# Four-layer hybrid decoder trunk: giving dense blocks out by recently streamed columns, merging over all columns, and moving one gate tile

## The chip, the cores and the metric

The kernel runs on one core of one Trainium2 chip, as one launch. The metric is the device time of a launch in microseconds, the median of three runs; the profile is of one further execution. Engines are named as the profile names them: PE (TensorE matmuls), PEld (its weight loads), DVE (VectorE), ACT (ScalarE), POOL (GpSimd) and SP (SyncE, which issues all DMAs here).

## What is computed

16 learned meta tokens and 256 tokens of width 1024 pass through four layers. Each layer is a token mixer and a SwiGLU FFN (inner width 2816), each added to the residual after an RMS norm. The mixers are, in order, forgetting attention (FoX, 16 heads of 64), gated linear attention (GLA, 4 heads), gated DeltaNet (8 heads of 128) and FoX again. Everything is fp32. The two mixers that matter here, cut to their cores:

```python
def fox_attend(q, cq, qpos, k, v, ck, kpos):
    s = jnp.einsum('bqhd,bkhd->bhqk', q, k)
    s = jnp.where(kpos[None, :] <= qpos[:, None], s + cq[..., :, None] - ck[..., None, :], -jnp.inf)
    return jnp.einsum('bhqk,bkhd->bqhd', jax.nn.softmax(s, axis=-1), v)

def gdn_chunk(state, inputs):
    ...
    lower = jnp.einsum('bhtd,bhsd->bhts', kb, kh) * jnp.exp(jnp.where(strict, diff, -jnp.inf))
    t_mat = jnp.eye(C) + lower
    sol = lax.linalg.triangular_solve(t_mat, rhs, left_side=True, lower=True, unit_diagonal=True)
    ...
```

After the DeltaNet's chunks each head's output is normed and multiplied by `silu(gate)`, then projected by `w_out`.

## The kernel before

Activations lie transposed, features on partitions and the 272 tokens as columns, in eight tiles of 128 features. A **dense block** is a 128x128 piece of a weight matrix times one such tile. Each fp32 operand is split in two fp32r parts (`wh`, `wl` of a weight; `zh`, `zl`, `ah`, `al`, `oh`, `ol` of an activation), and a block is three fp32r matmuls of 272 columns: `block`, L551. Eight blocks are a **weight unit**: `make_unit` (L573) issues its DMA on SP's queue, ACT copies it to `wh`, DVE subtracts to get `wl`; three units are held. An output tile of a mixer's input projection is eight blocks, one unit, 24 matmuls; the order of tiles is also the order of units in the packed weight array (`pack_weights`, `_in_cols`). Everything that is not dense (norm sums, scores, solves) is plain fp32 matmul, which the profile shows as two records each.

The order of work is made by a **planner**, the class `Trunk`, which runs in Python while the program is built and gives every engine its instruction order. It keeps its own clock `now` for PE. Tasks are generators; at a `yield` of tiles a task sleeps until the planner expects these tiles, and a `yield` of an event until it is set. `turn` (L470) picks what PE does next: if `warm` is false, dense blocks come first (`step`, L506); otherwise the first task that is ready, and a dense block only when no task is. `step` takes blocks of up to three open output tiles, whose weight units must be among the three held, and opens the next tile in a fixed order when a PSUM bank is free; it stops at a tile whose event is not set. `pe` (L398) records each PE instruction, advances `now` and, at the end of each planner tick (`TICK`, 3.413 us), sets `warm` by the columns counted in the tick (`> 3060`); while it is not warm an instruction is costed at double. `mm` (L412) counts an fp32 matmul as four times its columns, times the share of 128 rows that it uses, and an fp32r matmul as its columns times that share; it issues the instruction at L419. `tr` (L422) issues transposes at L424. PE instructions keep the planner's order on the chip; so if PE is sent an instruction whose operand isn't there yet, everything behind it waits. DVE, ACT and POOL instructions are placed by `Lane` (L260 in the profile).

**FoX, `attend` (L932).** One call per pair of heads, eight per FoX layer. It takes four PSUM banks for the scores, applies the softmax on DVE and ACT (`sm`, `mn`, `pr`, `su`, `ri`), transposes the probabilities on PE, copies them out (ACT to `pts`, DVE to `pt2`), and multiplies them with `vsb` into the bank `po`; ACT copies `po` to `osb`, which the gate task (`gate_done`, L1009) waits for. Between the second head's transposes and the matmuls of `po` (L993) the task does not pause.

**DeltaNet, `gdn` (L1328).** The 33 input tiles follow `GDN_ORDER` (L34): keys `k` 0 to 7, gates `r` 0 to 4, queries `q` 0 to 3, values `v` 0 and 1, `r` 5 to 7, `v` 2 and 3, then `q` and `v` 4 to 7 (a tile with decay and beta comes ahead of them). Tiles from place 19 on, other than gates, wait for `in_ev` (L1750). That event is set by `inverse` (L1517): a substitution of 15 steps on DVE (`tmp`, `gx`), transposes and copies give the inverses of 16x16 diagonal blocks of the chunk's triangle, `xm` and `xt`. `merge` (L1558) joins these to inverses of the whole chunk, for 4 heads and one of three chunks (96, 96 and 80 tokens) per call: first pairs of 16-blocks into 32-blocks, then 32 into 64 and 64 into the chunk, each step a few small fp32 matmuls with an ACT or DVE operation between. The three calls of heads 0 to 3 run first, then those of heads 4 to 7. In the first step only the half of the columns that can change is computed (`half`, L1570), 48 of 96 or 32 of 64, both products in one PSUM bank. `solve(i)` (L1676) waits for its head's merges, query and value, at most three heads at once; `wrap`, `gated` and `out_norm` follow, then the output projection. A gate tile `r` is evicted by DVE to `sr`, goes through Silu on ACT (`r_done`, L1737) and is read by `gated` after its head's solve.

Of the kernel before, what the change touches and what calls it, by code (L numbers as in the profile page):

```python
# [9 lines left out]
F32R = mybir.dt.float32r  # L10
# [23 lines left out]
GDN_ORDER = (  # L34
    [("k", i) for i in range(8)]
    + [("r", i) for i in range(5)]
    + [("q", i) for i in range(4)]
    + [("v", i) for i in range(2)]
    + [("r", i) for i in range(5, 8)]
    + [("v", i) for i in range(2, 4)]  # L40
    + [(c, i) for c in "qv" for i in range(4, 8)]
)
OUT_WIDE = 6
KEPT = ("_const_", "_z_", "_wraw_", "_wsp_", "_ps_")

# [33 lines left out]
def out_order(kind):  # L79

    if kind != "gdn":
        return [(i, k) for i in range(KD) for k in range(KD)]
    return [
        (i, k)
        for i0, i1 in ((0, OUT_WIDE), (OUT_WIDE, KD))
        for k0 in (0, KD // 2)
# [24 lines left out]
class Cols:  # L111

    def __init__(self):
        self.parts, self.at, self.n = [], {}, 0
# [193 lines left out]
class Trunk:  # L309
# [4 lines left out]
    RAWS = 3  # L314
    LAT = 0.14
    TICK = 3.413

    def __init__(self, tc, io, pcols, ccols, layers):
        self.tc, self.nc, self.io = tc, tc.nc, io
        self.pcols, self.ccols, self.layers = pcols, ccols, layers  # L320
        self.v = Lane(self, self.nc.vector, 0.1, 1 / 960.0)
        self.s = Lane(self, self.nc.scalar, 0.13, 1 / 1200.0)
        self.g = Lane(self, self.nc.gpsimd, 0.1, 2.4 / 1000.0)
        self.written, self.last, self.held = {}, {}, {}
        self.oh, self.ol, self.oh_ready = [None] * KD, [None] * KD, False
        self.issued, self.loaded, self.read, self.ended = 0.5, 0.0, [0.0] * self.RAWS, [0.0] * self.WBUFS
        self.now, self.seq = 0.0, 0
        self.tick, self.cols, self.warm = 0, 0, False
        self.tasks, self.bg, self.open = [], [], []
        self.banks, self.freed = 0, []  # L330
        self.nblock, self.units, self.nunit, self.used, self.first = 0, {}, 0, {}, 0
        self.prev = None
        self.begun, self.late, self.taken, self.epoch = set(), [], [], 0.0
# [64 lines left out]
    def pe(self, ins, cost, cols, aps, ready):  # L398
        if self.prev is not None:
            self.behind(ins.ins, self.prev)  # L400
        self.follow(ins.ins, aps, self.prev)
        self.prev = ins.ins.name
        self.now = max(self.now, ready)
        tick = int(self.now / self.TICK)
        if tick != self.tick:
            self.warm = tick == self.tick + 1 and self.cols > 3060
            self.tick, self.cols = tick, 0
        self.cols += cols
        self.now += cost if self.warm else 2 * cost
        self.touch(aps[0], self.now + 0.07, True)  # L410

    def mm(self, out, lhsT, rhs, start=True, stop=True, share=1.0):  # L412
        n = out.free_size()
        if lhsT.dtype == F32R:
            cost = max(0.1, n / 2400.0 + 0.003)
        else:
            n *= 4
            cost = max(0.07 + 0.0009 * lhsT.free_size(), n / 2400.0 + 0.003) * share
        ins = self.nc.tensor.matmul(out, lhsT, rhs, start=start, stop=stop)  # L419
        self.pe(ins, cost, n * rhs.shape[0] / 128, (out, lhsT, rhs), max(self.done_at(lhsT), self.done_at(rhs)) + self.LAT)  # L420

    def tr(self, out, in_):  # L422
        n = in_.shape[0]
        ins = self.nc.tensor.transpose(out, in_, self.con("ident")[:n, :n])  # L424
        self.pe(ins, 0.11, n, (out, in_), self.done_at(in_) + self.LAT)

    def go(self, gen):
        self.tasks.append([self.now, self.seq, gen, None])
# [41 lines left out]
    def turn(self):  # L470

        soon = []
        if not self.warm and self.step(soon):
            return True
        for t in self.tasks:
            at, ev = t[0], t[3]
            if ev is not None:
                if ev.t is None:
                    continue
                at = max(at, ev.t)  # L480
            if at > self.now:
                soon.append(at)
                continue
            try:
                r = next(t[2])
            except StopIteration:
                self.tasks.remove(t)
                return True
            t[0], t[3] = self.now, None
            if isinstance(r, Ev):  # L490
                t[3] = r
            elif isinstance(r, float):
                t[0] += r
            else:
                for a in r if isinstance(r, tuple) else (r,):
                    t[0] = max(t[0], self.done_at(a) + self.LAT)
            return True
        if self.step(soon):
            return True
        soon += [t for t in self.freed if t > self.now]  # L500
        if not soon:
            return False
        self.now = max(self.now, min(soon)) + 1e-6
        return True

    def step(self, soon):  # L506
        while True:
# [185 lines left out]
    def add_out(self, z, evs, nk, gain, lo=0, store=False, order=None):  # L693
# [17 lines left out]
        if order:  # L711
            places = {ik: self.nblock + n for n, ik in enumerate(order)}
            for i in range(KD):
                self.bg.append(Dense([places[i, k] for k in range(KD)], z, evs, lo, done(i), OUT_WIDE))
            self.nblock += KD * KD
# [112 lines left out]
    def fox(self, j, lo, gain):  # L828
# [9 lines left out]
        with ExitStack() as cx:  # L838
# [93 lines left out]
            def attend(jp):  # L932
# [10 lines left out]
                for hh in range(2):  # L943
                    r, hd = R[hh], 2 * jp + hh
# [24 lines left out]
                pts, pt2 = [], []  # L969
                for hh in range(2):  # L970
                    pt = yield from self.bank()
                    for i3, (a, b) in enumerate(qt):
                        for k3 in range(i3 + 1):
                            t0, n = TILES[k3]
                            src = pr[hh][: b - a, offs[i3] + t0 : offs[i3] + t0 + n]
                            if k3 == 0:
                                dst = pt[:n, a:b]
                            elif k3 == 1:
                                dst = pt[:n, T + a - 96 : T + b - 96]
                            else:  # L980
                                dst = pb[hh][:n, T : T + 80]
                            self.tr(dst, src)
                    x = tp.tile([96, 448], F32, tag="pts", name="pts")
                    x2 = tp.tile([80, 80], F32, tag="pt2", name="pt2")
                    s.activation(x[:, lo:], pt[:96, lo:448], AF.Copy)
                    v.tensor_copy(x2, pb[hh][:80, T : T + 80])
                    self.free(pt)
                    self.free(pb[hh])
                    pts.append(x)
                    pt2.append(x2)  # L990
                    if hh == 0:
                        yield pr[1]
                po = yield from self.bank()  # L993
                for i3 in range(3):
                    for hh in range(2):
                        r = R[hh]
# [331 lines left out]
    def gdn(self, j, lo, gain):  # L1328
# [5 lines left out]
        with ExitStack() as cx:  # L1334
# [223 lines left out]
            def merge(grp, i3):  # L1558

                yield in_ev  # L1560
                t0, n = TILES[i3]
# [3 lines left out]
                xtn, xmn, ymn = xtg[:n, :, :n], xmg[:n, :, :n], ym[:n, :, :n]  # L1565
                m = 16
                nn = n // 32 * 32
                nh = nn // 2

                def half(a, hf):  # L1570
                    return a[..., :nn].rearrange("p (n x c) -> p n x c", x=2, c=m)[:, :, hf, :]

                p = yield from self.bank()
                for i in range(4):
# [3 lines left out]
                    half_mask[:n, None, :n].to_broadcast([n, 4, n]), ALU.mult)  # L1578
                self.free(p)
                yield ym  # L1580
                p = yield from self.bank()
                for i in range(4):
                    self.mm(p[:n, i * 96 : i * 96 + nh], xtn[:, i], half(ymn[:, i], 0))
                    self.mm(p[:n, i * 96 + 48 : i * 96 + 48 + nh], ymn[:, i], half(xtn[:, i], 1))
                pv = p[:n, :384].rearrange("p (h x c) -> p h x c", h=4, x=2)
                for hf, a in ((0, xmn), (1, xtn)):
                    av = a[:, :, :nn].rearrange("p h (n x c) -> p h n x c", x=2, c=m)[:, :, :, hf, :]
                    sv = pv[:, :, hf, :nh].rearrange("p h (n c) -> p h n c", c=m)
                    v.tensor_tensor(av, av, sv, ALU.add)
                self.free(p)  # L1590
                yield xmg, xtg
                e2 = n - 64
                p = yield from self.bank()
                pv = p[:, :128].rearrange("p (h c) -> p h c", h=4)
# [5 lines left out]
                p = yield from self.bank()  # L1600
                pv = p[:, :128].rearrange("p (h c) -> p h c", h=4)
# [7 lines left out]
                p = yield from self.bank()  # L1609
                pv = p[:, :256].rearrange("p (h c) -> p h c", h=4)  # L1610
# [5 lines left out]
                p = yield from self.bank()  # L1616
                pv = p[:, : 4 * e2].rearrange("p (h c) -> p h c", h=4)
# [239 lines left out]
```

## Time and profile before

| what | us |
|---|---|
| median of 3 runs (1547.57 to 1555.5) | 1552.88 |
| the profiled execution | 1550.78 |
| its span, first to last instruction | 1549.0 |
| PE busy in it | 1498.8 |
| DVE busy, ACT busy | 1092.3, 781.8 |

The mean granted clock of PE over the span is 0.983; 1.00 is 2.4 GHz and 0.50 is 1.2 GHz. A busy time of PE counts a matmul from start to modelled end; since matmuls overlap, distances from start to start tell more than the mean duration of one. In windows, a number behind an engine is its busy time in the stretch, with the count of its instructions in brackets. The stages lie, in us: FoX 0 to 160, SwiGLU to 397, GLA to 540, SwiGLU to 745, DeltaNet to 969, SwiGLU to 1190, FoX to 1328, SwiGLU to the end.

### The profile page before, as it was taken

What the parts mean: (1) busy time and instruction counts of PE and PEld (TensorE: products, weight loads), DVE (VectorE), ACT (ScalarE), POOL (GpSimd) and SP (SyncE); (2) the same over time, 40 slices, a digit from 0 to 9 for tenths busy, and PEclk for the clock granted to TensorE, in tenths of its full rate; (3) what the DMA queues carried; (4) which work ended last, traced back from release to release, by engine and by line L of the source; (5) the groups of instructions that cost most, each with busy time, mean ns of one, the idle gap of its engine ahead of it and who ended that gap; (6) DMA issues with size and microseconds to landing.
All of it is one profiled execution on the core that took longest, in us unless ns stands there. A gap on an engine that the chain in (4) does not pass through costs nothing.

```text
span 1549.0 us, 29524 instructions
## 1 busy us (share of the span) xinstructions
PE 1498.8 (97%) x11985; PEld 1453.4 (94%) x11985; DVE 1092.3 (71%) x2161; ACT 781.8 (50%) x1418; POOL 18.1 (1%) x58
## 2 busy tenths in 40 slices
PE   7899999999999999999898998999999999999999
PEld 7888999999999999999897897999999888999999
DVE  7778776665796876655979476866656778786653
ACT  6556554444445544444675354544445556654442
POOL 0000000000000000000200000000000000000000
PEclk9999999999999999999998897999999999999999
DMA  5232455555433455555333021455554333455564
GB/s 192 98 107 96 156 178 175 177 177 177 145 102 106 144 187 168 175 178 175 112 122 109 21 86 65 161 178 172 177 172 163 110 111 108 136 191 189 184 199 138
DMA packets 63737, 225.25 MB, mean 145 GB/s; under 512 B 7232, under 2 KB 9632, under 8 KB 63600
## 3 DMA queue, kind: packets, MB, share of 16 engines
q1 hardware_dynamic: 63600, 223.36, 43.3%
q8 instruction: 94, 1.54, 0.4%
q14 instruction: 43, 0.35, 0.1%
HBM read 222.28 MB, written 1.05 MB: 144 GB/s over the span
## 4 chain that ended last, share of the span: by engine, by line
PE 82%; DVE 11%; ACT 4%; issue 1%; DMA 1%; SPq 0%; DVEq 0%; ACTq 0%
PE ps L419 82%; DVE wl L260 3%; ACT pr L260 1%; ACT wh L260 1%; DVE rq L260 1%; DMA w<-in_w_dram 1%; DVE pr L260 1%; DVE sm L260 1%; PE ps L424 1%; DVE k L260 1%; ACT pts L260 0%; DVE ri L260 0%; DVE yc L260 0%; SPq L392 0%; DVE d L260 0%
## 5 line engine op out<-in xcount | busy, mean ns | idle before, releaser
L419 PE MATMUL ps<-zh,wh 128*128 128x272 f32 (+1 forms) x2400 | 711.2, 296 | 8.2 <-ACT zh L260 6.8
L419 PE MATMUL ps<-zh,wl 128*128 128x272 f32 (+1 forms) x2400 | 693.4, 289 | 3.1 <-DVE wl L260 3.1
L419 PE MATMUL ps<-zl,wh 128*128 128x272 f32 (+1 forms) x2400 | 695.0, 290 | 0.0
L260 ACT ACTIVATE wh<-w 128x1024 fp32r<-128x1024 f32 x420 | 443.1, 1056 | 384.3 <-PE ps L419 191.6
L260 DVE TENSOR_TENSOR wl<-w,wh 128x1024 fp32r<-128x1024 f32 x420 | 512.2, 1221 | 161.4 <-ACT wh L260 161.1
L419 PEld LDWEIGHTS ps<-zh,wh 128*128 128x128 f32 x2400 | 456.6, 190 | 17.2 <-ACT zh L260 6.7
L419 PEld LDWEIGHTS ps<-zh,wl 128*128 128x128 f32 x2400 | 456.7, 190 | 6.0 <-DVE wl L260 4.4
L419 PEld LDWEIGHTS ps<-zl,wh 128*128 128x128 f32 x2400 | 456.3, 190 | 0.0
L419 PE MATMUL ps<-al,wh 128*128 128x272 f32 (+1 forms) x704 | 202.0, 287 | 0.0
L419 PE MATMUL ps<-ah,wl 128*128 128x272 f32 (+1 forms) x704 | 201.4, 286 | 0.0
L419 PE MATMUL ps<-ah,wh 128*128 128x272 f32 (+1 forms) x704 | 201.0, 285 | 0.0
L419 PEld LDWEIGHTS ps<-ah,wh 128*128 128x128 f32 x704 | 133.1, 189 | 0.0
L419 PEld LDWEIGHTS ps<-al,wh 128*128 128x128 f32 x704 | 132.4, 188 | 0.0
L419 PEld LDWEIGHTS ps<-ah,wl 128*128 128x128 f32 x704 | 132.2, 188 | 0.0
L260 DVE TENSOR_TENSOR s<-t,rs 128x272 f32<-128x272 f32 (+1 forms) x88 | 38.5, 437 | 64.9 <-ACT t L260 64.8
L260 DVE TENSOR_TENSOR al<-a,ah 128x272 fp32r<-128x272 f32 (+1 forms) x88 | 38.6, 438 | 64.4 <-ACT ah L260 64.3
L419 PE MATMUL ps<-oh,wh 128*128 128x272 f32 (+1 forms) x256 | 75.6, 295 | 1.2 <-ACT wh L260 1.2
L419 PE MATMUL ps<-oh,wl 128*128 128x272 f32 (+1 forms) x256 | 74.7, 292 | 1.0 <-DVE wl L260 0.9
L419 PE MATMUL ps<-ol,wh 128*128 128x272 f32 (+1 forms) x256 | 74.7, 292 | 0.1
L260 ACT ACTIVATE ah<-a 128x272 fp32r<-128x272 f32 (+1 forms) x88 | 36.8, 418 | 62.9 <-DVE a L260 62.9
L260 ACT ACTIVATE zh<-h,par 128x272 fp32r<-128x272 f32 x64 | 32.7, 519 | 67.7 <-DVE h L260 66.5
L260 ACT ACTIVATE pr<-sm,mn 96x192 f32<-96x192 f32 (+3 forms) x96 | 42.2, 441 | 26.3 <-DVE mn L260 26.2
(225 smaller groups left out, 1511.7 us busy)
## 6 DMA issues: line engine op xcount, KB each, us to landing
w<-in_w_dram SPq DMA_DIRECT2D x420, 512.0 KB, 3.3
h<-in_h_dram SPq DMA_DIRECT2D x4, 272.0 KB, 5.2
out_dram<-h SPq DMA_DIRECT2D x8, 128.0 KB, 3.3
mask<-in_fmask_dram SPq DMA_DIRECT2D x2, 210.0 KB, 5.0
con<-in_con_dram SPq DMA_DIRECT2D x1, 207.5 KB, 6.0
mask<-in_gmask_dram SPq DMA_DIRECT2D x1, 126.0 KB, 2.1
par<-in_par_dram SPq DMA_DIRECT2D x1, 87.5 KB, 3.1
half<-in_dmask_dram SPq DMA_DIRECT2D x1, 36.0 KB, 1.7
```

What stands on the lines that cost most here:

```text
L260: r = f(*args, **kw)
L419: ins = self.nc.tensor.matmul(out, lhsT, rhs, start=start, stop=stop)
L424: ins = self.nc.tensor.transpose(out, in_, self.con("ident")[:n, :n])
```

## The change

Five edits in one. (2) What `mm` and `tr` count is now weighted by the part of the 128x128 array that is used, and an fp32 matmul counts six times its columns rather than four. (3) `turn` gives dense blocks the first place not only when `warm` is false, but also when the work counted over the last tick's length of planner time is not above 2950. (4) `attend` pauses until the planner expects the copies of the transposed probabilities. (5) `merge` computes its first step over all columns, the two products in two PSUM banks; and gate tile 7 of the DeltaNet goes from its place behind `r` 6 to the end of the order.

```diff
-    + [("r", i) for i in range(5, 8)]
+    + [("r", i) for i in range(5, 7)]
     + [("v", i) for i in range(2, 4)]
     + [(c, i) for c in "qv" for i in range(4, 8)]
 )
+GDN_ORDER[31:31] = [("r", i) for i in range(7, 8)]
...
+    KEEP = 2950
+    NEAR = 2950
...
-            self.warm = tick == self.tick + 1 and self.cols > 3060
+            self.warm = tick == self.tick + 1 and self.cols > self.KEEP
             self.tick, self.cols = tick, 0
         self.cols += cols
+        self.recent = [x for x in self.recent if x[0] > self.now - self.TICK] + [(self.now, cols)]
...
     def mm(self, out, lhsT, rhs, start=True, stop=True, share=1.0):
         n = out.free_size()
+        work = n * rhs.shape[0] * lhsT.free_size() / 128**2 * (1 if lhsT.dtype == F32R else 6)
...
-        self.pe(ins, cost, n * rhs.shape[0] / 128, (out, lhsT, rhs), max(self.done_at(lhsT), self.done_at(rhs)) + self.LAT)
+        self.pe(ins, cost, work, (out, lhsT, rhs), max(self.done_at(lhsT), self.done_at(rhs)) + self.LAT)
...
-        self.pe(ins, 0.11, n, (out, in_), self.done_at(in_) + self.LAT)
+        self.pe(ins, 0.11, 2 * n * n * in_.free_size() / 128**2, (out, in_), self.done_at(in_) + self.LAT)
...
-        if not self.warm and self.step(soon):
+        if not self.busy() and self.step(soon):
             return True
...
+    def busy(self):
+
+        return self.warm and sum(c for t, c in self.recent if t > self.now - self.TICK) > self.NEAR
...
                     if hh == 0:
                         yield pr[1]
+                yield tuple(pts + pt2)
                 po = yield from self.bank()
...
-                p = yield from self.bank()
+                ps = yield from self.bankn(2)
                 for i in range(4):
-                    self.mm(p[:n, i * 96 : i * 96 + nh], xtn[:, i], half(ymn[:, i], 0))
-                    self.mm(p[:n, i * 96 + 48 : i * 96 + 48 + nh], ymn[:, i], half(xtn[:, i], 1))
-                pv = p[:n, :384].rearrange("p (h x c) -> p h x c", h=4, x=2)
+                    self.mm(ps[0][:n, i * 96 : i * 96 + nn], xtn[:, i], ymn[:, i, :nn])
+                    self.mm(ps[1][:n, i * 96 : i * 96 + nn], ymn[:, i], xtn[:, i, :nn])
                 for hf, a in ((0, xmn), (1, xtn)):
-                    av = a[:, :, :nn].rearrange("p h (n x c) -> p h n x c", x=2, c=m)[:, :, :, hf, :]
-                    sv = pv[:, :, hf, :nh].rearrange("p h (n c) -> p h n c", c=m)
+                    av, sv = (
+                        t[:, :, :nn].rearrange("p h (n x c) -> p h n x c", x=2, c=m)[:, :, :, hf, :]
+                        for t in (a, ps[hf][:n, :384].rearrange("p (h c) -> p h c", h=4)))
                     v.tensor_tensor(av, av, sv, ALU.add)
-                self.free(p)
+                    self.free(ps[hf])
                 yield xmg, xtg
```

## Rows read from the trace of the kernel before

**Rows 1.** The page: busy time of PE, and the chain that ended last by engine.

```profile
PE 1498.8 (97%) x11985; PEld 1453.4 (94%) x11985; DVE 1092.3 (71%) x2161; ACT 781.8 (50%) x1418; POOL 18.1 (1%) x58
...
PE 82%; DVE 11%; ACT 4%; issue 1%; DMA 1%; SPq 0%; DVEq 0%; ACTq 0%
```

**Rows 2.** Windows by stage: length, busy us and count per engine, granted clock, DMA share, GB/s.

```profile
0.00:160.00 160.00, 142.40 (x1109) 128.92 (x1109) 124.04 (x373) 92.41 (x228) 0.51 (x5) 0.99 0.37 123
160.00:397.00 237.00, 237.00 (x1881) 236.84 (x1881) 156.32 (x235) 114.13 (x164) 3.49 (x7) 1.00 0.52 174
397.00:540.00 143.00, 138.29 (x1130) 134.21 (x1129) 116.01 (x196) 75.82 (x130) 4.01 (x9) 1.00 0.37 121
...
745.00:969.00 224.00, 205.93 (x1598) 191.92 (x1597) 163.19 (x378) 117.71 (x267) 1.85 (x19) 0.89 0.25 82
...
1190.00:1328.00 138.00, 131.20 (x1061) 118.54 (x1060) 108.45 (x342) 80.76 (x208) 0.00 (x0) 1.00 0.33 110
```

**Rows 3.** Windows at changes of the granted clock, DeltaNet stretch (same columns).

```profile
849.55:856.37 6.82, 6.82 (x46) 6.27 (x45) 3.66 (x9) 2.88 (x6) 0.20 (x2) 0.50 0.00 0
887.10:897.33 10.23, 10.23 (x74) 8.97 (x72) 3.59 (x8) 3.50 (x9) 0.10 (x1) 0.50 0.22 72
934.89:948.50 13.61, 13.26 (x48) 11.38 (x49) 7.66 (x18) 5.98 (x20) 0.00 (x0) 0.50 0.24 78
...
846.10:849.50 3.40, 2.62 (x43) 2.56 (x44) 3.40 (x10) 2.09 (x6) 0.10 (x1) 1.00 0.02 5
883.70:887.10 3.40, 3.40 (x53) 2.99 (x53) 1.42 (x4) 0.79 (x3) 0.00 (x0) 1.00 0.02 5
...
926.00:934.90 8.90, 6.47 (x46) 5.26 (x45) 8.38 (x19) 5.12 (x12) 0.00 (x0) 1.00 0.19 60
```

**Rows 4.** Waits of PE, PEld, whole span: total us, times, longest us.

```profile
PE ps L419 <- ACT pts L260: 8.2, 16, 1.3
...
PE ps L419 <- DVE xm L260: 6.6, 1, 6.6
...
PE ps L419 <- DVE ym L260: 0.9, 1, 0.9
...
PEld ps L419 <- ACT pts L260: 15.6, 32, 1.8
```

**Rows 5.** Chain that ended last, DeltaNet stretch: start us, us, what.

```profile
830.81 0.44 DVE sr L260
...
837.39 6.93 PE ps L419 x42
...
846.88 20.59 PE ps L419 x202
...
894.62 25.23 PE ps L419 x182
```

**Rows 6.** Chain that ended last, end of the second FoX stretch.

```profile
1302.30 1.22 DVE wl L260
...
1322.38 0.42 ACT pts L260
```

**Rows 7.** PE's instructions by line and form, 900 to 928 us.

```profile
L419 PE MATMUL ps<-zh,wh 128*128 128x272 f32 x51 | 15.7, 307 | 0.0
```

**Rows 8.** Timeline of PE, merges at full clock: start us, us, instruction, count.

```profile
868.74 0.84 PE L419 MATMUL ps<-xm,l 96*96 96x96 f32 x8
...
871.38 0.33 PE L419 MATMUL ps<-xt,ym 96*96 96x48 f32 x2
...
872.40 0.33 PE L419 MATMUL ps<-xt,ym 96*96 96x48 f32 x2
```

**Rows 9.** Windows, end of the DeltaNet stretch (columns as in rows 2).

```profile
928.00:969.00 41.00, 35.65 (x194) 31.44 (x193) 27.31 (x62) 16.98 (x45) 0.00 (x0) 0.79 0.20 65
```

**Rows 10.** Timeline of PE, dense matmuls in the first slow piece (first and last of 15).

```profile
851.83 0.59 PE L419 MATMUL ps<-zh,wh 128*128 128x272 f32 x1
...
855.17 0.43 PE L419 MATMUL ps<-zl,wh 128*128 128x272 f32 x1
```

More of the change, by code (lines that the diff above doesn't have):

```diff
@@ L327, in __init__ @@
         self.now, self.seq = 0.0, 0
-        self.tick, self.cols, self.warm = 0, 0, False
+        self.tick, self.cols, self.warm, self.recent = 0, 0, False, []
         self.tasks, self.bg, self.open = [], [], []
@@ L1567, in merge @@
                 nn = n // 32 * 32
-                nh = nn // 2
-                def half(a, hf):
-                    return a[..., :nn].rearrange("p (n x c) -> p n x c", x=2, c=m)[:, :, hf, :]
                 p = yield from self.bank()
```

## The prediction

> **What bounds the kernel now.** The page comes first [rows 1]: the PE rows fill 97% of the span and the chain that ended last lies 82% on PE, so the question is where PE's order or clock wastes time. The windows by stage [rows 2] answer it: the first SwiGLU stretch has PE busy all of its 237 us at full clock (the other three look the same), while both FoX stretches leave PE idle (17.6 of 160 us, 6.8 of 138 us) and the gated-delta stretch, 745 to 969 us, is idle for 18.1 of 224 us at a granted clock of 0.89. Only these can give much back.
>
> In the delta stretch the windows show three long pieces at a granted clock of 0.50, half of 2.4 GHz [rows 3]: 849.55 to 856.37, 887.10 to 897.33 and 934.89 to 948.50 us. (A fourth follows the wait for the inverse's `xm`, 6.6 us [rows 4], and is due to that.) Ahead of the third PE was busy for only 6.47 of 8.90 us, waiting on solves. But the first two come out of small work: 846.10 to 849.50 us holds 43 matmuls and the wait of 0.9 us for `ym` [rows 4], 883.70 to 887.10 holds 53 and no idle time at all, most of them narrow merge matmuls. The clock fell there while PE had ready work. The chain [rows 5] runs through PE for 20.6 us from 846.88 on and again for 25.2 us from 894.62 on, so these two pieces cost real time: (6.82 + 10.23) / 2 = **8.5 us** against the same order at full clock.
>
> In FoX, PE waits for the copies `pts` 16 times, 8.2 us in all on the matmuls (15.6 us if the weight loads' waits are taken) [rows 4]. Each of the 16 `attend` calls gives out its output matmuls right behind the transposes, before the copy that they read is done; everything behind them in PE's order waits too.
>
> **The extra pause in attend (L993).** Nothing is added on the chip: the same instructions and semaphores, but the planner now hands PE other work until the copies are due. If there are dense blocks, the whole 8.2 us is filled; at most 15.6. But the end of a FoX stretch is not always PE's: from 1302 to 1322 us the second one's chain is DVE and ACT work, with the splits `wl` of 1.2 us among it [rows 6]. Time won before the last group's query and key tiles counts, what is won in the last group (2 of 8 calls) does not: 8.2 x 6/8 = **6.1 us**. Bounds 0 (the filling blocks wait for their own `wl` instead) and 15.6. What moves later is the output matmul, then `osb`, the gate and the output projection; in the body of a stretch nobody waits for these.
>
> **The new rule in turn (busy, recent, weights in mm and tr).** No work is added; dense blocks change places. Before, blocks came ahead of ready tasks only after a whole planner tick with few columns; now also when the last tick's length of planned PE work falls below 2950, where a narrow fp32 matmul counts little (a 32x32x32 one 12, against 32 before) and a full-width one counts 6 a column instead of 4. In the delta stretch that puts blocks between the merges, 843 to 900 us, in place of 900 to 928 us, where 153 dense records stand in one piece [rows 7]. A block is three matmuls 0.126 us apart (237 us hold 1881) [rows 2]. The nearest rows say what it earns: the first two pieces at clock 0.50, **8.5 us**. Below: 0, if the clock stays as it is; above: 8.5 plus half of the last piece's 13.61, 15.3 us [rows 3]. I take 8.5, since these two pieces have the pattern at which the rule aims. SwiGLU stretches have only dense work to give out; the GLA stretch has granted clock 1.00 throughout [rows 2]; 0 there, and PE's full columns hide it.
>
> **Merges over all columns.** 48-column merge matmuls start 0.085 us apart ((872.40 - 871.38) / 12), and eight 96-column ones with weights of the same width take 0.84 us with their tail, (0.84 - 0.25) / 7 = 0.084 us apart [rows 8]. Doubling the columns thus costs 0; the cover is the weight load, 96 columns in both. If it were gone, the four merges of 96 (8 matmuls of two records each, 64 records) would grow by 48 columns at 2 cycles of 2.4 GHz, 2.6 us, and the two of 80 (32 records, 32 columns) by 0.9 us: bound 3.5 us, taken 0. DVE adds the same elements from two banks. Each merge now wants two of eight PSUM banks at once: no row prices this, the nearest wait is 0.9 us for `ym` [rows 4], so 0 to 6 x 0.9 = 5.4 us; I take 0, because a PE full of other work hides such a wait. A gain needs a reason that I don't see.
>
> **Last gate tile at the end.** Moved are 24 matmuls (3.0 us), one weight load on SP's queue, its `wh` on ACT and `wl` on DVE (1.22 us [rows 6]), the eviction `sr` on DVE (0.44 us [rows 5]) and a Silu on ACT; nothing on POOL. It passes ten tiles, whose loads and splits each come one unit earlier on SP, ACT and DVE. The chain shows the price of its present place: PE works until 830.8 us on just this tile, DVE evicts it (830.81 us) and only then goes on with the substitution whose result PE awaits until 837.39 [rows 5]. Without it the inverse ends earlier by at least the 0.44 us, with the `wl` out of the way too by 1.7: taken **0.6**, near the lower end, as another tile's split will mostly stand there instead. PE idles some 3 us longer before the inverse, which costs nothing as DVE's substitution sets that end. The 3.0 us return later; 928 to 969 us is idle for 41 - 35.65 = 5.4 us and at clock 0.79 [rows 9], which holds them: 0 (bound 3.0). Who reads `sr` of head 7 comes only after its solve, so the late Silu delays nobody.
>
> **Sum.** 6.1 + 8.5 + 0.6 = 15.2 us off the profiled execution's 1550.8 us (span 1549.0 and 1.8 around it) gives 1535.6. The median shown, 1552.9, is 2.1 above that execution; I forecast **1537 us** in medians.
>
> One rule speaks against the largest term. Ahead of the second piece PE shows no idle time, ahead of the first less than 0.8 us [rows 3], and yet the clock is halved. The Trainium skill (TensorE: Matmul & The Clock Gate, "HAM oscillation") says that it is PE's idle gaps, such as waits for a DMA, that throttle the clock again. By that rule blocks between busy merges would earn nothing, and the sum would be 6.7 instead of 15.2 us. The trace sides against it for the second piece; where long waits stand ahead of a piece it agrees.
>
> **Rivals.**
> 1. *The clock is not regained.* The planner's time drifts from the chip's, so that the blocks fall elsewhere, or the merges are too dense in small matmuls. For it: even now the planner puts 15 dense matmuls into the first piece, one after another [rows 10], and it stays at 0.50 to its end [rows 3]. Against: the GLA stretch, small matmuls with dense blocks between, has clock 1.00 [rows 2]. Gain 6.1 + 0.6: 1546 us. The clock rule of the Trainium skill (same page and section) would give this time too.
> 2. *FoX gives nothing.* The pause's blocks run into `wl`, since in the second FoX stretch DVE is busy 108 of 138 us [rows 2] and its chain ends on DVE. Gain 8.5 + 0.6: 1544 us.
> 3. *The merges come late: slower.* Blocks are given out ahead of the merges on which solves 4 to 7 wait. If all 153 records of 900 to 928 us go first, with the gate tile's 24, that is 177 x 0.126 = 22.3 us more ahead of the last merge, less 8.5 of clock: 13.8 us later. It decides if the solves behind them cannot be shortened, because their own waits on PE, ACT and DVE set their pace; then 900 to 928, stripped of dense work, also falls to the 0.79 of the stretch behind it [rows 9], 28 x 0.21 = 5.9 us more. With FoX's gain: 1553 + 13.8 + 5.9 - 6.7 = 1566 us. Against: solves 4 to 7 need the same query and value tiles, which then come sooner.
> 4. *Nothing moves*, what is won in one place returns as a wait in the next: 1553 us.
> 5. *More.* The last slow piece goes as well and FoX gives all 15.6: 15.6 + 15.3 + 0.6 = 31.5: 1521 us.
>
> **How the numbers follow.** Forecast 0.42 (its own range 1529 to 1545), rival 1 0.15, rival 2 0.13, rival 3 0.12, rival 4 0.10, rival 5 0.08. About 0.5% (7.8 us) is what a measurement of this kernel can tell from no change, so faster is below 1545 and slower above 1561. Faster: 0.95 of the forecast, 0.35 of rival 1, 0.6 of rival 2, all of rival 5: 0.40 + 0.05 + 0.08 + 0.08 = 0.61. Slower: rival 3, 0.12. The rest, 0.27, is the same. The range leaves out about a tenth at either end: from 1523, near rival 5, to 1558, past rival 4 but short of rival 3.
>
> **What would show it.** In the changed profile, the wait of PE for `pts` should fall from 8.2 us to under 2; the windows of the delta stretch should show dense records between the merges with a granted clock near 1.0 from 843 to 900 us; PE's wait for `xm` should be longer than 6.6 us while `xm` itself comes about 0.6 us sooner; merge rows should read 96x96 at an unchanged count, and `sr` should have its last eviction after 920 us. The prediction is wrong if those waits are gone and the FoX stretches are no shorter (then DVE sets them), if slow pieces stand where PE is full, or if the last solve ends later after the last merge than now.

## The result and the profile after

| | before | changed |
|---|---|---|
| median of 4 runs, us | 1554.19 (1547.57 to 1557.22) | 1530.86 (1527.45 to 1534.97) |
| the profiled execution, us | 1550.78 | 1527.45 |
| its span, us | 1549.0 | 1525.6 |
| its mean granted clock | 0.983 | 0.990 |

The ratio is 0.9857, with a 95% interval from 0.9811 to 0.9902: faster by 1.4%, some 22 us, and 6 us below the forecast of 1537, inside its range. The same changed kernel was measured again later and gave 0.9879 (0.9850 to 0.9908).

The page of the changed kernel, busy time and the chain by engine (they answer to [rows 1]):

```profile
PE 1480.7 (97%) x11985; PEld 1440.2 (94%) x11985; DVE 1094.2 (72%) x2161; ACT 779.7 (51%) x1418; POOL 17.8 (1%) x58
...
PE 86%; DVE 9%; ACT 3%; issue 1%; DMA 1%; SPq 0%; ACTq 0%; DVEq 0%
```

The counts of PE, DVE, ACT and POOL are those of before; PE is busy 18.1 us less, and the chain lies on it for 86% in place of 82%. The same work is done in another order and, in part, at a higher clock.

To place the gain by stage, two groups of matmuls serve as marks. `ps<-nacc,con` is the norm sum in front of a layer half: its first start lies at the first FoX, its last behind the second. `ps<-nacc,sel` is the norm sum over heads in the GLA layer (first start) and in the DeltaNet layer (last start). PE's timeline by tile: ns min/median/max, first and last start in us. Before:

```profile
L419 PE MATMUL ps<-nacc,con x16: 391/392/433, 17.2 to 1363.3; 128*128 128x272 f32 x16
L419 PE MATMUL ps<-nacc,sel x16: 283/288/574, 499.1 to 964.5; 128*128 128x272 f32 x16
```

Changed:

```profile
L424 PE MATMUL ps<-nacc,con x16: 391/392/412, 16.8 to 1339.9; 128*128 128x272 f32 x16
L424 PE MATMUL ps<-nacc,sel x16: 283/288/596, 492.6 to 947.4; 128*128 128x272 f32 x16
```

The stretch with the first FoX shrinks from 499.1 - 17.2 = 481.9 us to 475.8 (6.1 us gained), that with the DeltaNet from 465.4 to 454.8 (10.6 us), that with the second FoX from 398.8 to 392.5 (6.3 us). Inside the DeltaNet the gain is uneven. From the norm sum that follows the SwiGLU ahead of it (738.01 us before, 731.76 after) to the transposes of the decay (`rr`, 757.62 and 754.75) **3.4 us are lost**; from there to the DeltaNet's last norm sum 14.2 us are gained.

What PE waited for in the changed kernel, in us, times, longest (compare [rows 4]):

```profile
PE ps L424 <- DVE xm L261: 5.9, 1, 5.9
PE ps L429 <- DVE rr L261: 5.5, 1, 5.5
PE ps L424 <- DVE wl L261: 5.4, 7, 1.5
...
PE ps L424 <- ACT pts L261: 0.2, 1, 0.2
...
PEld ps L424 <- ACT pts L261: 1.2, 4, 0.4
```

The waits for `pts` are all but gone, on the matmuls and on the weight loads. Waits for `wl` have risen a little (3.9 us in four waits before), and that for `rr` from 3.5 to 5.5 us.

Windows of the changed kernel's DeltaNet stretch, columns as in [rows 2]:

```profile
829.40:843.00 13.60, 8.30 (x50) 7.91 (x51) 11.35 (x23) 8.90 (x16) 0.20 (x2) 0.50 0.13 39
843.00:900.00 57.00, 56.81 (x590) 50.62 (x589) 35.63 (x94) 27.60 (x75) 0.80 (x8) 1.00 0.12 38
900.00:928.00 28.00, 28.00 (x221) 27.45 (x221) 25.48 (x55) 17.20 (x39) 0.00 (x0) 1.00 0.31 103
928.00:952.00 24.00, 20.54 (x126) 18.64 (x125) 15.92 (x35) 9.81 (x26) 0.00 (x0) 0.86 0.28 88
```

Here both pieces of [rows 3] are gone: 843 to 900 us is at full clock. But this window does not show where the dense matmuls went, for the merges now end at 889.64 us (898.65 before), and what stands behind them falls into it. From the first merge matmul to the last, PE's instructions of one form, before (837.39 to 898.70 us, first fence) and after (833.04 to 889.70 us, second):

```profile
L419 PE MATMUL ps<-zh,wh 128*128 128x272 f32 x24 | 10.5, 439 | 0.0
```

```profile
L424 PE MATMUL ps<-zh,wh 128*128 128x272 f32 x18 | 6.1, 339 | 0.0
```

A block has one record of this form among its three: 72 dense records stood between the merges, 54 stand there now. **The changed kernel has fewer dense blocks between its merges, not more.** Of the 18 records 15 now lie ahead of the first merge (from the transposes of the decay to it, 136 records of this form before and 133 now, although gate tile 7 with its 8 is gone from there).

So this one profile reads like the prediction come true in the clock, but not in the order. The experiments show that the clock, too, flatters the new order.

### The profile page after: what moved, and what is told of

Same layout as the page of the kernel before. It is cut to its first block, busy times and chain, and to the rows that moved or that the text cites. A ratio compares the mean times of both kernels' runs of the same rounds, so it can differ in the third digit from the quotient of the medians.

```text
span 1525.6 us, 29516 instructions
## 1 busy us (share of the span) xinstructions
PE 1480.7 (97%) x11985; PEld 1440.2 (94%) x11985; DVE 1094.2 (72%) x2161; ACT 779.7 (51%) x1418; POOL 17.8 (1%) x58
## 4 chain that ended last, share of the span: by engine, by line
PE 86%; DVE 9%; ACT 3%; issue 1%; DMA 1%; SPq 0%; ACTq 0%; DVEq 0%
PE ps L424 85%; DVE wl L261 2%; ACT pr L261 1%; PE ps L429 1%; DVE pr L261 1%; DVE rq L261 1%; ACT wh L261 1%; DVE sm L261 1%; DVE k L261 1%; DVE ri L261 1%; DMA w<-in_w_dram 0%; DVE nacc L261 0%; DMA h<-in_h_dram 0%; DVE l1p L261 0%; DVE b L261 0%
## 5 line engine op out<-in xcount | busy, mean ns | idle before, releaser
L424 PEld LDWEIGHTS ps<-zh,wh 128*128 128x128 f32 x2400 | 454.8, 190 | 16.9 <-ACT zh L261 6.3
```

## The experiments

**How they are read.** The 66 executions of the kernel before that ran beside the experiments, on four chips (means 1549.8 to 1550.2 us), lie between 1540.3 us at a mean clock of 0.990 and 1562.7 us at 0.975, mean 1550.0. Most of this spread is the clock: the time that PE spent at half clock, 2 x (1 - mean clock) x span, averages 49.5 us, and over the executions the time grows by 0.42 us for each us of it. So the table gives, beside the ratio of medians, the change of the mean time against 1550.0, the change of the half-clock time against 49.5, and the change of the rest (the time less half of the half-clock time; 1525.2 before), which is a measure, if a rough one, of an order's worth apart from the clock. All in us, with intervals of 95%; "alone" is the kernel before with one edit, "without" is the changed kernel with one undone.

| label | kernel | ratio of medians | time | half clock | rest |
|---|---|---|---|---|---|
| a_pause | pause alone | 0.9900 (0.9878 to 0.9922) | -14.9 ± 2.4 | -12.7 ± 5.2 | -8.5 ± 1.9 |
| a_rule | rule alone | 0.9986 (0.9959 to 1.0012) | -2.9 ± 3.4 | -1.3 ± 6.0 | -2.3 ± 1.3 |
| a_merge | merges alone | 1.0025 (0.9994 to 1.0055) | +5.0 ± 2.3 | +8.0 ± 8.1 | +1.0 ± 2.2 |
| a_gate | gate tile alone | 0.9975 (0.9949 to 1.0000) | -2.5 ± 4.3 | +3.4 ± 8.7 | -4.2 ± 1.5 |
| b_pause | without pause | 0.9977 (0.9955 to 1.0000) | -4.0 ± 2.9 | -1.3 ± 7.8 | -3.3 ± 1.5 |
| b_rule | without rule | 0.9928 (0.9901 to 0.9954) | -10.5 ± 3.0 | -0.3 ± 6.4 | -10.3 ± 2.5 |
| b_merge | without merges | 0.9914 (0.9892 to 0.9936) | -13.7 ± 1.1 | +0.3 ± 3.0 | -13.9 ± 1.2 |
| b_gate | without gate tile | 0.9908 (0.9877 to 0.9940) | -14.5 ± 5.8 | -2.7 ± 13.6 | -13.1 ± 1.5 |
| c_after | changed kernel again, with the first 4 runs | 0.9879 (0.9850 to 0.9908) | -19.0 ± 2.7 | -10.0 ± 7.7 | -14.0 ± 1.3 |
| c_cols | merges alone, order held | 1.0028 (1.0001 to 1.0056) | +3.3 ± 4.2 | +2.0 ± 10.0 | +2.3 ± 1.2 |
| c_pool | changed kernel, memsets later | 0.9848 (0.9820 to 0.9876) | -23.9 ± 3.7 | -18.0 ± 8.8 | -14.9 ± 1.0 |
| d_near | c_pool, bound 4000 | 0.9905 (0.9876 to 0.9933) | -16.1 ± 4.1 | -7.6 ± 8.7 | -12.3 ± 0.7 |

The ratio in the row of c_after is that of its own runs; the other columns take both sets.

**Which edit earns the time.** Two theories stood against each other: the forecast's, in which the DeltaNet edits (rule, merges, gate tile) earn more than the pause, and its rival, in which the pause carries the gain. Four kernels have one edit alone, four leave one out.

a_pause puts the pause into the kernel before, b_pause takes it out of the changed one:

```diff
+                yield tuple(pts + pt2)
                 po = yield from self.bank()
```

a_pause. 

> The pause alone, on the kernel before. If the FoX gain is the pause's own: the two FoX stretches shorten by 6.0 and 6.6 us as they do in the changed kernel, PE's wait for pts falls from 8.2 to under 1 us, the DeltaNet stretch keeps its slow pieces (51 us at clock 0.50 in all), time about 12.5 us below before. Rival, that the new counting also moved the FoX order: under 7 us.

b_pause. 

> The changed kernel without the pause. If parts add up: 12.5 us above the changed kernel (1531), so about 1543, with pts waits back at 8 us; DeltaNet as in the changed kernel. If the pause also pays in the DeltaNet (another start state of the planner), more than 15 us.

a_rule has the rule alone, with `KEEP`, `NEAR`, `recent` and `work`; b_rule is the changed kernel with all of it undone:

```diff
-        if not self.warm and self.step(soon):
+        if not self.busy() and self.step(soon):
```

a_rule. 

> The new counting and the rule in turn alone, on the kernel before. If the rule regains the clock in the merges: slow pieces in 843 to 900 us gone, 4 to 8 us of DeltaNet gained, FoX unchanged (pts still 8 us). Rival, that the merges' extra columns keep the clock up: both slow pieces stay, under 2 us.

b_rule. 

> The changed kernel with the old counting and the old rule in turn. If the rule regains the clock in the merges: the slow pieces of 843 to 900 us come back (17 us at 0.50) and the time is 5 to 9 us above the changed kernel. Rival, that full columns and the gate tile carry the DeltaNet's gain: within 3 us of it.

a_merge has the merges over all columns alone, b_merge goes back to `half`:

```diff
-                p = yield from self.bank()
+                ps = yield from self.bankn(2)
...
+                    self.mm(ps[0][:n, i * 96 : i * 96 + nn], xtn[:, i], ymn[:, i, :nn])
+                    self.mm(ps[1][:n, i * 96 : i * 96 + nn], ymn[:, i], xtn[:, i, :nn])
```

a_merge. 

> Merges over all columns alone, on the kernel before. If the columns themselves keep the clock up: at least one of the two slow pieces in 843 to 900 us goes and the merges end 4 to 5 us earlier; merge matmuls still start 0.085 us apart. If the rule does it: slow pieces stay, time within 2 us of before. A slower result by over 2 us would mean that the two banks are waited for.

b_merge. 

> The changed kernel with half-column merges in one bank. If the rule alone keeps the clock: within 2 us of the changed kernel and no slow piece between 843 and 900. Rival, that the columns do it: slow pieces back there, 4 to 8 us above.

a_gate has gate tile 7 at the end alone, b_gate puts it back:

```diff
-    + [("r", i) for i in range(5, 8)]
+    + [("r", i) for i in range(5, 7)]
...
+GDN_ORDER[31:31] = [("r", i) for i in range(7, 8)]
```

a_gate. 

> The last gate tile at the end alone, on the kernel before. As predicted: the first merge starts 0.6 to 1.5 us earlier after the start of the decay work, PE waits longer for xm (over 8 us), and the last slow piece (13.6 us ahead of the end) shortens because 24 dense matmuls stand there: 1 to 4 us in all. Rival, that the tile is given out before the tail: 0.6 to 1.5 us only and the last slow piece unchanged.

b_gate. 

> The changed kernel with gate tile 7 back in its old place. If the tile fills the tail: the slow piece ahead of the end of the DeltaNet stretch grows back from 6.8 towards 13.6 us and the first merge comes 1.5 us later, 2 to 5 us above the changed kernel. Rival: the tail's gain comes from the earlier merges and the tile gives its 0.6 us only: within 1.5 us.

Measured: the pause alone takes 14.9 us off, the other edits together 4.0; the sum, 18.9, is the whole change's 19.0. **The pause carries the gain.** The marks say where. a_pause:

```profile
L419 PE MATMUL ps<-nacc,con x16: 390/392/432, 17.4 to 1347.8; 128*128 128x272 f32 x16
L419 PE MATMUL ps<-nacc,sel x16: 283/288/392, 493.3 to 955.8; 128*128 128x272 f32 x16
```

b_pause:

```profile
L424 PE MATMUL ps<-nacc,con x16: 390/392/423, 19.6 to 1353.0; 128*128 128x272 f32 x16
L424 PE MATMUL ps<-nacc,sel x16: 283/288/392, 502.3 to 954.2; 128*128 128x272 f32 x16
```

With the pause alone the FoX stretches are 475.9 and 392.0 us long: 6.0 and 6.8 gained. Without it they are 482.7 and 398.8, as before. In all eight profiles with the pause the second stretch lies between 391.9 and 393.2 us, in all six without it at 398.7 or above. And a_pause's waits are those of the changed kernel:

```profile
PE ps L419 <- ACT pts L260: 0.2, 1, 0.2
...
PEld ps L419 <- ACT pts L260: 1.2, 4, 0.4
```

a_pause's rest, -8.5, is less than the 12.8 us of its two FoX stretches. The pause shifts the planner's clock, and with it the places of dense blocks in the DeltaNet too; whether that order is worse or the rest is too rough a measure, these runs don't tell.

Alone, none of the three DeltaNet edits has a ratio whose interval lies below 1; in the rest, the order's part, the rule (-2.3) and the gate tile (-4.2) do gain. The merges alone are, by the means, slower, but not in the rest (+1.0 ± 2.2), so nothing shows that their two banks are waited for. Left out of the changed kernel, the rule costs 8.5 ± 3.4 us and the merges 5.3 ± 2.6; the gate tile's 4.5 ± 5.6 is not clear of nothing. These add up to more than the 4.0 that the three bring together, but the excess lies in the half-clock time, which is 9.7, 10.3 and 7.3 us higher without them: in the rest they cost 3.7, 0.1 and 0.9 us, 4.7 in all, near the 5.5 by which the changed kernel's rest lies below a_pause's. Why the half-clock time rises in all three, these runs don't settle.

**Whether the clock's gain is the order's.** The theory: dense blocks between the merges hold the clock up. The rival: whether a piece falls to half clock is chance. c_after is the changed kernel itself; c_cols gives PE the full columns in the order of before, by telling the planner the old number of columns (on top of a_merge's edit):

```diff
-    def mm(self, out, lhsT, rhs, start=True, stop=True, share=1.0):
-        n = out.free_size()
+    def mm(self, out, lhsT, rhs, start=True, stop=True, share=1.0, n=None):
+        n = n or out.free_size()
...
+                    self.mm(ps[0][:n, i * 96 : i * 96 + nn], xtn[:, i], ymn[:, i, :nn], n=nn // 2)
```

c_after. 

> The changed kernel once more, for more executions. Each execution of one kernel so far cost about half a microsecond more for every microsecond at clock 0.50, so both parts are read from all executions: time less half the slow time, and slow time. If the DeltaNet edits gain through the clock: slow time at most 42 us on average where the kernel before has 50, and the rest 13 to 14 us lower than before. Rival, that the first four executions were lucky in the clock: slow time as before, gain 13 to 15 us in all.

c_cols. 

> The kernel before with full-column merges in two banks, but with the planner's counts of the half-column ones, so that PE's order stays as it was and only the streamed columns differ. If more columns keep the clock up: slow time down by 8 us or more, time down by about 4. Rival (only idle time lowers the clock): slow time and time as before within 2 us.

Measured, windows of c_after's profiled execution (1536.47 us):

```profile
833.60:864.30 30.70, 28.22 (x212) 25.75 (x212) 17.89 (x44) 15.82 (x35) 0.61 (x6) 0.50 0.11 35
865.00:900.00 35.00, 34.81 (x349) 30.54 (x346) 18.34 (x53) 13.07 (x46) 0.20 (x2) 1.00 0.07 23
```

The same instructions in the same order ran at half clock for 30.7 us, where the first profile shows 13.6; the stretch between the `nacc,sel` marks is 463.9 us long in place of 454.8 (465.4 before). So the 10.6 us that the first profile shows in the DeltaNet stretch are for the most part that execution's: in c_after the same order gains 1.5 us there. Over ten executions the half-clock time is down by 10.0 ± 7.7 us, worth somewhat less than half of that in time. That it is the DeltaNet edits which do this is not shown: b_pause has all of them and -1.3 ± 7.8 us, a_pause has none and -12.7 ± 5.2. And the theory has its premise against it. Of all profiles, a_rule's has the most dense records between the merges, 3 x 30, and the lowest clock from the first to the last of them:

```profile
L423 PE MATMUL ps<-zh,wh 128*128 128x272 f32 x30 | 13.4, 447 | 0.0
...
843.93:921.70 77.77, 74.20 (x606) 66.33 (x606) 43.33 (x113) 32.75 (x85) 0.91 (x9) 0.74 0.11 35
```

So dense blocks between the merges do not by themselves hold the clock up; what does stays open. The merges' matmuls show the two levels, PE's timeline of the first profile and of c_after:

```profile
843.08 0.33 PE L424 MATMUL ps<-xt,ym 96*96 96x96 f32 x2
843.25 0.33 PE L424 MATMUL ps<-ym,xt 96*96 96x96 f32 x2
843.42 0.33 PE L424 MATMUL ps<-xt,ym 96*96 96x96 f32 x2
```

```profile
843.24 0.53 PE L424 MATMUL ps<-xt,ym 96*96 96x96 f32 x2
...
845.16 0.53 PE L424 MATMUL ps<-xt,ym 96*96 96x96 f32 x2
```

Two records take 0.17 us from start to start in the first, 0.085 each: 96 columns cost what 48 did [rows 8]. In c_after the twelve records between the two lines are 1.92 / 12 = 0.16 us apart, just under twice as far (so are a_rule's of 48 columns at half clock). c_cols gains nothing, so full columns by themselves do not hold the clock up.

**The 3.4 us lost at the DeltaNet's start.** In the changed kernel DVE's timeline shows one instruction out of all proportion, beside POOL's (start us, us, instruction). Changed kernel, DVE, then POOL:

```profile
731.24 0.43 DVE L261 TENSOR_SCALAR nacc<-con 128x272 fp32r<-128x272 f32 x1
731.62 1.23 DVE L261 TENSOR_TENSOR wl<-w,wh 128x1024 fp32r<-128x1024 f32 x1
732.76 4.38 DVE L261 TENSOR_SCALAR nacc<-con 128x272 fp32r<-128x272 f32 x1
```

```profile
731.45 1.13 POOL L261 MEMSET gx<- 96x1056 f32 x1
...
732.70 2.09 POOL L261 MEMSET xm<- 96x768 f32 x3
734.73 2.10 POOL L261 MEMSET xt<- 96x768 f32 x3
```

The second zeroing of `nacc` took 4.38 us where its twin took 0.43, exactly while POOL zeroed `xm` and `xt`. Theory: POOL's row of memsets keeps DVE out; rival: the slow record is harmless and `rr` is late for another reason. c_pool moves these memsets behind the wait for the keys; PE's order stays.

```diff
-                for t in xm + xt:
-                    g.memset(t, 0.0)
                 for e in ks_ev:
                     yield e
+                for t in xm + xt:
+                    g.memset(t, 0.0)
```

c_pool. 

> The changed kernel with POOL's zeroing of xm and xt issued after the key tiles rather than ahead of them; PE's order is the same. If POOL's row of memsets holds up DVE's zeroing of a helper tile at the end of the second SwiGLU stretch (4.38 us there): that instruction takes under 0.9 us, the decay transposes come about 3 us earlier, time 2 to 3.5 us below the changed kernel run beside it. Rival, that DVE is held by something else: still over 4 us, time within 1 us.

Measured, DVE's timeline of c_pool:

```profile
737.14 0.29 DVE L261 TENSOR_SCALAR nacc<-con 128x272 fp32r<-128x272 f32 x1
```

The instruction is back at 0.29 us, PE waits 3.6 us for `rr`, and from the norm sum to `rr` it is 19.8 us in place of 23.0 (c_after 22.3, before 19.6). The theory holds: this row of memsets is what keeps DVE out. The other profiles agree: where the longest `nacc<-con` took 3.4 to 4.4 us (a_pause, a_rule, a_gate, c_cols, c_after and the first profile), PE waited 5.5 or 5.6 us for `rr`; in the others that instruction took at most 1.5 us and the wait was 4.1 us or less. But the collision is not the change's doing. c_cols has PE's order of the kernel before and lost as much (22.9 us to `rr`), and in the kernel before itself the two instructions lie just as far apart, DVE's timeline, then POOL's:

```profile
739.01 0.83 DVE L260 TENSOR_SCALAR nacc<-con 128x272 fp32r<-128x272 f32 x1
```

```profile
738.95 2.40 POOL L260 MEMSET xm<- 96x768 f32 x3
```

In nine profiles the instruction starts 0.06 or 0.07 us behind the first of the six memsets; it took 0.83 us in three of them, 1.51 in two, 3.54 in one (c_after) and 4.38 in three (the first profile, a_rule and a_gate). How many memsets go ahead of DVE is thus not set by these starts, and what sets it stays open. Behind the wait for the keys they cannot meet.

c_pool beats both kernels in median, 1524.9 us. Against the kernel before that is certain; against the changed kernel the difference of means, 4.9 us, lies mostly in the half-clock time and the intervals of the two ratios overlap, so the 3.2 us at the start are shown and the gain at the end is not.

**How far the blocks can go.** The slower rival says that blocks ahead of the merges make the last solves late. d_near raises the bound below which blocks go first.

```diff
-    NEAR = 2950
+    NEAR = 4000
```

d_near. 

> The kernel with POOL's zeroing moved (1524.9 us), with NEAR = 4000 in place of 2950: PE's order differs in the DeltaNet stretch alone, with more dense blocks between the merges. If dense blocks between merges keep the clock: slow time below the 31 us of that kernel, time 1518 to 1523 us. If whether the piece behind the wait for xm lasts is chance: slow time 30 to 45 us, time 1524 to 1531. If more blocks make the merges late: time less half the slow time over 1512 us, where it is 1510.

Measured: 16.1 us off the kernel before, 7.8 less than c_pool. The rest is 2.6 ± 1.0 us worse, and the traces show most of it at the rival's place: with 3 x 23 dense records between the merges in place of 3 x 18, it is 59.2 us from first to last merge in place of 56.9. (The order differs in the second FoX as well, but that stretch is as long, 392.6 and 392.8 us.) From the last merge to the last solve's output it is 52.6 us in place of 48.8, but here d_near has a piece at half clock that c_pool has not:

```profile
926.10:932.90 6.80, 6.80 (x27) 6.33 (x27) 4.18 (x10) 3.60 (x12) 0.00 (x0) 0.50 0.22 80
```

Half of 6.8 us is 3.4 of these 3.8, so that part is the execution's. The rival's mechanism is real, then, at some 2 us, and the changed kernel, with fewer dense records between the merges than before, stays short of it: there the last solve's output comes 48.8 us after the last merge, where before it came after 56.4 (898.65 to 955.01 us), 13.6 us of which were at half clock [rows 3].

## Why the prediction was right, and where it was not

The forecast, 15.2 us off (from 1552.9 that makes 1537.7, which the prediction rounds down to 1537), stands against 19.0 ± 2.7 over ten executions and 22 in the first runs. The total was right by luck, through two errors that go against each other: the FoX term is some 6 us too small, the DeltaNet's terms are some 5 us too large.

**The pause: mechanism right, term too small.** Forecast 6.1 us from 8.2 x 6/8, measured 12.4 us by the marks in the changed kernel (6.1 + 6.3) and 12.8 in a_pause (6.0 + 6.8). The step that failed is the choice between the two rows of the wait: the matmuls' 8.2 us was taken where the weight loads' 15.6 was the better one, 15.6 x 6/8 = 11.7. More was gained than the whole 8.2, so no share of that row could have given it, and of the loads' 32 waits half don't show in the matmuls' 16. The likely reason, argued and not tested: a matmul's end is modelled, so a stall hides behind the drawn end of the matmul before it, and the load's wait does not. The part for the last group of heads was half right: in the first FoX 7.1 us were gained by the first score matmul of the last group and 6.0 by the norm sum behind it, so nothing in that group, as forecast; in the second it was 4.3 and 6.3. Rival 2, blocks that run into `wl`, came true by at most the 1.5 us that these waits rose (2.2 in the weight loads' row).

**The rule: mechanism not borne out, term too large.** Forecast 8.5 us. Two steps failed. That blocks come to stand between the merges is so with the rule alone (a_rule has 90 dense records there, the kernel before 72); with the merges over all columns, which the planner counts as more work, fewer are given out (a_merge has 48), and the changed kernel has 54. And the price took two half-clock pieces of one execution for a property of the order that such blocks would end: a_rule, with the most of them, has the lowest clock there. In the first profile of the changed kernel both pieces went; in c_after, the same order, a longer one stood in their place, as in the rival "the clock is not regained". In b_pause, where only the three DeltaNet edits work, they are worth 4.0 ± 2.9 us; the forecast's terms for them make 9.1, that rival's 0.6. What the rule gains apart from the clock (2.3 us of rest alone, 3.7 inside the change) the prediction did not have, and where it comes from stays open.

On the clock rule of the Trainium skill (TensorE: Matmul & The Clock Gate, "HAM oscillation"), that PE's idle gaps throttle the clock: c_after's long piece agrees at its start, for in the 7.60 us ahead of it PE was busy for 2.51:

```profile
826.00:833.60 7.60, 2.51 (x20) 2.29 (x19) 7.15 (x18) 2.15 (x4) 0.00 (x0) 1.00 0.20 74
```

It does not tell its length: PE was then busy for 28.22 of 30.70 us and stayed at half clock, while the same order came back to full clock after 13.6 us in the other execution, with PE busy for only 8.30 of them (there the piece began 3.6 us ahead of the first merge, in c_after 0.8). Full clock in one and half in the other, for the same instructions, is what these runs show; what decides between them stays open.

**Merges: 0 forecast, right within the bounds as a price, incomplete as an account.** Columns cost nothing and no matmul waits for `ym` any more (0.9 us in [rows 4]). The edit alone is slower by 5.0 ± 2.3 us in means; inside the change it earns 5.3 ± 2.6. The rest shows neither (+1.0 ± 2.2 alone, 0.1 inside), so both lie in the clock, and the prediction had it there only in the term for the rule.

**Gate tile: 0.6 forecast, too small to be told.** From `rr` to the first merge it is 79.8 us before, 78.3 in the changed kernel and 77.9 in a_gate. But c_after, the changed kernel again, takes 79.9, and c_cols, with PE's order of before, 78.3: executions of one order differ there by 1.5 us, nearly the bound of 1.7. The eviction of the last gate tile moved where it was put. Changed kernel, DVE by tile:

```profile
L261 DVE TENSOR_TENSOR sr<-ps,rs x8: 428/432/442, 776.7 to 927.7; 128x272 f32<-128x272 f32 x8
```

PE's wait for `xm` was to grow beyond 6.6 us. It did in a_gate (7.8 us) and not in the changed kernel (5.9 us), where the rule puts blocks in front of it (3.6 us in a_rule).

**Left out:** the 3.4 us at the start of the DeltaNet. No step looked for a collision of POOL and DVE. It is no price of the change, though: the kernel before can meet it too.

## What to carry to other kernels

Read a stall of PE from the weight loads' row of the waits, not from the matmuls', before it is priced. To see what an order puts into a stage, count from the stage's first instruction to its last in each kernel; a window of fixed times takes in what has moved behind it. Ask of every term whether the thing it removes would be there in another execution: a piece at half clock may not be, a wait set by the order of instructions is, and the two should stand apart in the comparison (time less half of the half-clock time). Look for long rows of POOL memsets beside DVE's work, and put them where DVE's next result is not awaited.

## What the runs showed of the hardware that was not expected

- A DVE instruction of 0.43 us stood for 4.38 us through a row of six POOL memsets of about 0.7 us each. The Trainium skill (SBUF — State Buffer, "Who interferes with whom") says that DVE's second port pair is GpSimd's too, that operations such as `tensor_scalar` can want it, and that the loser is blocked until the other's instruction ends. The row agrees that it was blocked, but for the whole row of memsets, not for one; in the kernel before, with the same starts, the block ended with the first memset (0.83 us). The `wl` subtraction with two operands kept its 1.23 us beside POOL's earlier memsets, as that section says of an operation with two inputs next to a GpSimd one that only writes.
- The clock can fall with PE busy all the while (883.70 to 887.10 us [rows 3]), and the length of a half-clock piece differs by a factor of two between executions of one program (13.6 and 30.7 us). Of the kernel before, executions differ by 22 us, 1.4%, mostly by this.
